# First projection of a two-layer decoder trunk as a fixed pipeline, with the later conditioning loads on GpSimd's queue

## The chip, the cores and the metric

The kernel runs on one core of one Trainium2 chip. The metric is the time of one execution on the device in microseconds (us). Three runs of the kernel before took 687.07, 687.56 and 693.68 us, with a median of 687.56.

## The reference

Two decoder layers work on x of 256 tokens by 1024 features, in float32. The vector c is passed through silu and multiplied by a 1024 x 6144 matrix of each layer (`ada_w`), which gives that layer's six conditioning vectors: shift, scale and gate for the mixer and for the feed-forward part. Cut to what matters here:

```python
mod = silu(c) @ ada_w[layer] + ada_b[layer]          # 6 vectors of 1024
h = rmsnorm(x, mix_pre_g[layer]) * (1.0 + scale_m) + shift_m
proj = h @ w_in                                       # layer 0: q, k, v of 16 heads
y = mixer(proj) @ w_out                               # layer 0 adds rel_bias to its scores
x = x + gate_m * rmsnorm(y, mix_post_g[layer])
h = rmsnorm(x, ffn_pre_g[layer]) * (1.0 + scale_f) + shift_f
u = causal_conv3(h @ w_up) + conv_b
y = (gelu(u_gate) * u_val) @ w_down
x = x + gate_f * rmsnorm(y, ffn_post_g[layer])
```

Layer 0 has eight softmax heads of kind A and eight of kind B, layer 1 eight latent heads (C) and eight stick-breaking heads (D).

## The kernel before

Every projection is computed in float32 quality from three products of float32r parts: a weight tile is loaded as it is (`raw`), ScalarE rounds it to a high part (L315) and VectorE subtracts that for a low part (L316). The activations are kept as `hh` and `hl` (features by tokens), and TensorE forms w_high·hh, w_low·hh and w_high·hl. So each weight passes DMA, ScalarE, VectorE and TensorE in turn.

The **first projection** (q, k and v of the A heads, 1024 x 1536 weights) runs over four slices of 256 input rows (`SLICES`). For a slice, `ada_first` multiplies silu(c) with the shift and scale columns of that slice alone (L154), ScalarE copies the sums out, four transposes (L232) turn them into columns, and three small VectorE operations (L235 to L238) finish the vectors A and B; then `h_part` writes `hh` (L367) and `hl` (L373) from transposed x, and the products L819 (q, k) and L323 to L325 (v) follow. The weights of `ada_first` are 2.1 MB a slice, those of the projection 1.57 MB. Tiles of tag `aw` (four of them, 512 KB each) hold conditioning weights, both for the slices and for everything later; tag `raw` has four tiles, tag `qkv` eight.

Behind the first projection the kernel forms the bias table of the scores (L830 to L838: a transpose, a product, an addition, a store to memory as `bias_d`), copies q, k and v out, and loads and turns the conv vectors `vec_b` (L851 to L857). Then come attention A, whose softmax (`soften`, L587) reads `bt` tiles loaded from `bias_d` (L864), the projection of the B heads (L477, L323 to L325), attention B, the output projection (y0m), a `boundary` with norms (m0), the feed-forward part, and layer 1 in the same manner. The remaining conditioning vectors are placed in this sequence by `ADA_AT`: kind "p" on TensorE (`ada_cols`, `ada_gate`), kind "v" on VectorE (`ada_vector`, two operations for each 512 KB tile), with the loads of each in `ada_load` (L143). The norms' reciprocal square roots (`rstd_halves`, L339 and L340), the masks of the D heads (L676) and some rotary arithmetic (L971, L972, L1025) are GpSimd's (POOL).

**Order.** A planner (`schedule_with_timeline_sim`) orders each engine's queue by simulated times, with program order as the priority. `manual_schedule` keeps the instructions of a block in written order on the engines named, but others may be planned between them; `issue_after(ins)` puts an instruction behind another on the same engine. Up to `in_order.close()` (L858) SyncE's (SP's) DMA issues stay in written order. An issue that waits for a free tile holds back what stands behind it in its queue.

Of the kernel before, what the change touches and what calls it, by code (L numbers as in the profile page):

```python
# [17 lines left out]
P = 128  # L18
# [47 lines left out]
def trunk_kernel(  # L66
# [70 lines left out]
    mods, last_load, last_gelu, last_full, last_h, last_down, last_low, last_main = {}, [], [], [], [], [], [], []  # L137

    def ada_load(layer, c0, tag="aw"):
# [18 lines left out]
    def ada_part(layer, c0, ws):  # L158
        ps = bank(f"ada_{layer}_{c0}", "a")
        ada_main(ps, ws)  # L160
# [59 lines left out]
    def ada_first(i, before=0, behind=0):  # L220
# [3 lines left out]
        if before:  # L224
            keep_clock(before)
# [14 lines left out]
    def ada_first_load(i, u):  # L240
        k0, n = SLICES[i]
        w = tl("aw", [P, 2, 512], f"aw_first{i}_{u}")
# [6 lines left out]
    def ada_gate(layer, which, h, post_g, tag="aw", on="a", on_vector=False):  # L249
# [22 lines left out]
        ada_main(ps, ws)  # L272
# [505 lines left out]
    first_ws = {0: [ada_first_load(0, u) for u in range(2)]}  # L778
# [4 lines left out]
    rb = small("rb", (16, 32), tag="o")  # L783
    oh = small("oh", (32, TW), tag="o")
    bias = small("bias", (16, TW), tag="o")
    for dst, src in ((rb, rel_bias), (oh, k_onehot), (bias, k_reach)):
        nc.sync.dma_start(dst, src)
    first_ws[0] += [ada_first_load(0, u) for u in range(2, 4)]
    vT = turned(vec_a, P, "vT")
    ada_first(0, 9, 6)  # L790
    w_in = ab_w_in[0]
    qkv = qkv_tiles("a")
    pq, pk = y_tile("psa_q"), y_tile("psa_k")
    pv = [bank(f"psa_v{t}") for t in range(2)]

    for i, (k0, n) in enumerate(SLICES):
        w = w_in[k0 * P:(k0 + n) * P]
        raw_qk = tl("raw", [P, n, 1024], f"rawaqk_{i}")
        for k in range(n):
            nc.sync.dma_start(raw_qk[:, k, :], w[k * P:(k + 1) * P, 0:1024])  # L800
# [294 lines left out]
```

## Time and profile before

| | |
|---|---|
| median of 3 runs | 687.56 us (687.07 to 693.68) |
| profiled execution | 689.92 us, of which the span of the trace is 687.9 us |
| TensorE (PE) busy | 660.6 us, 96% of the span; mean granted clock 0.99 |
| VectorE (DVE) busy | 524.7 us, 76% |
| ScalarE (ACT) busy | 369.0 us, 54% |
| GpSimd (POOL) busy | 33.9 us, 5% |
| moved by DMA | 159.10 MB, 231 GB/s in the mean |
| chain that ended last | PE 82%, DMA 5%, DVE 4%, ACT 4% |

The profiled execution is one run of the kernel, and every duration below is from it. The table's shares are means over stages with different limits; the stages are shown one by one further down. A granted clock of 1.00 is TensorE's full level of 2.4 GHz, and a stretch below 1.00 was spent partly at the lower one, 1.2 GHz.

### The profile page before, as it was taken

To read this page: it belongs to the slowest core of one execution; us is meant where nothing else is said; L and a number is where in the kernel's file an instruction comes from. 1 tells how busy PE (TensorE), PEld (TensorE's weight loads), DVE (VectorE), ACT (ScalarE), POOL (GpSimd) and SP (SyncE) were. 2 spreads that over 40 slices of the span, in tenths; PEclk is the share of its full clock that TensorE was granted. 3 is DMA by queue.
4 is the path that set the end of the run, shared out by engine and by line. 5 is a ranking of instruction groups with operands and counts; after the bars stand their busy time and mean duration, and the time that the engine had idled before them with its cause. 6 is when DMAs were issued, how large, how long until landed. Compare 5 with 4: busy or idle time off the path is not lost.

```text
span 687.9 us, 11772 instructions
## 1 busy us (share of the span) xinstructions
PE 660.6 (96%) x4547; PEld 571.4 (83%) x4547; DVE 524.7 (76%) x1008; ACT 369.0 (54%) x645; POOL 33.9 (5%) x95
## 2 busy tenths in 40 slices
PE   7899999799999999999999999989999999999996
PEld 5778976376899999999986998667599999999995
DVE  1545578688899999999898796764788777777775
ACT  3434365645565555555555645865565555555552
POOL 2000000001000000000002002410200000000000
PEclk9999999899999999999999999999999999999998
DMA  7899999986858778888885867723166555555511
GB/s 257 283 349 390 276 340 292 303 304 221 291 191 290 273 254 306 264 260 277 271 291 185 268 227 269 231 87 106 54 193 237 184 183 184 184 185 188 191 50 61
DMA packets 100818, 159.10 MB, mean 231 GB/s; under 512 B 4087, under 2 KB 62611, under 8 KB 100763
## 3 DMA queue, kind: packets, MB, share of 16 engines
q1 hardware_dynamic: 100739, 158.35, 69.5%
q8 instruction: 35, 0.57, 0.4%
q14 instruction: 20, 0.16, 0.1%
q10 hardware_dynamic: 24, 0.02, 0.0%
HBM read 156.52 MB, written 1.84 MB: 230 GB/s over the span
## 4 chain that ended last, share of the span: by engine, by line
PE 82%; DMA 5%; DVE 4%; ACT 4%; issue 2%; POOL 1%; SPq 1%; DVEq 0%; POOLq 0%; ACTq 0%
PE u L477 33%; PE y1f L698 9%; PE y0f L698 7%; PE psb L477 3%; PE psd L477 3%; PE y1m L698 2%; DMA aw<-in_ada_w 2%; PE psa_q L819 2%; PE psa_k L819 2%; DMA aw_first<-in_ada_w 2%; PE y0m L698 2%; PE ada L154 2%; DMA rawd<-in_ffn_w_down 1%; PE ada_first L154 1%; ACT junknm L335 1%
## 5 line engine op out<-in xcount | busy, mean ns | idle before, releaser
L747 ACT ACTIVATE cv<-u,cvT 128x256 f32<-128x256 f32 x88 | 49.1, 561 | 62.9 <-PE u L477 59.1
L477 PE MATMUL u<-hh,wu_0h 128*128 128x256 f32 x352 | 69.9, 280 | 1.2 <-DVE hh L431 1.2
L477 PE MATMUL u<-hh,wu_1h 128*128 128x256 f32 x352 | 70.1, 280 | 0.0
L477 PE MATMUL u<-hh,wu_1l 128*128 128x256 f32 x352 | 69.9, 279 | 0.0
L477 PE MATMUL u<-hh,wu_0l 128*128 128x256 f32 x352 | 69.5, 279 | 0.0
L315 ACT CAST wu_1h<-rawu 128x1024 fp32r<-128x1024 f32 x44 | 46.3, 1053 | 31.1 <-PE y1f L698 17.6
L748 DVE SCALAR_TENSOR_TENSOR cv<-u,cvT,cv 128x255 f32<-128x255 f32 x88 | 42.1, 479 | 26.4 <-ACT cv L747 26.3
L199 DVE SCALAR_TENSOR_TENSOR acc<-aw,cpad,acc 128x512 f32<-128x512 f32 x77 | 57.8, 751 | 2.0 <-DMA aw<-in_ada_w 1.6
L477 PEld LDWEIGHTS u<-hh,wu_0h 128*128 128x128 f32 x352 | 54.8, 188 | 4.2 <-PE ada L276 1.4
L316 DVE TENSOR_TENSOR wu_0l<-rawu,wu_0h 128x1024 fp32r<-128x1024 f32 x44 | 53.6, 1222 | 5.3 <-ACT wu_0h L315 5.3
L315 ACT CAST wu_0h<-rawu 128x1024 fp32r<-128x1024 f32 x44 | 46.0, 1046 | 19.0 <-PE u L477 19.0
L316 DVE TENSOR_TENSOR wu_1l<-rawu,wu_1h 128x1024 fp32r<-128x1024 f32 x44 | 53.7, 1220 | 3.0 <-ACT wu_1h L315 3.0
L477 PEld LDWEIGHTS u<-hh,wu_1l 128*128 128x128 f32 x352 | 53.7, 188 | 0.0
L477 PEld LDWEIGHTS u<-hh,wu_1h 128*128 128x128 f32 x352 | 53.7, 188 | 0.0
L477 PEld LDWEIGHTS u<-hh,wu_0l 128*128 128x128 f32 x352 | 53.5, 188 | 0.0
L477 PE MATMUL u<-hl,wu_1h 128*128 128x256 f32 x352 | 48.2, 279 | 0.0
L477 PE MATMUL u<-hl,wu_0h 128*128 128x256 f32 x352 | 48.2, 279 | 0.0
L315 ACT CAST wd_0h<-rawd 128x1024 fp32r<-128x1024 f32 x26 | 27.3, 1049 | 36.8 <-PE u L477 30.2
L477 PEld LDWEIGHTS u<-hl,wu_1h 128*128 128x128 f32 x352 | 44.2, 188 | 0.0
L477 PEld LDWEIGHTS u<-hl,wu_0h 128*128 128x128 f32 x352 | 44.2, 188 | 0.0
L316 DVE TENSOR_TENSOR wd_0l<-rawd,wd_0h 128x1024 fp32r<-128x1024 f32 x26 | 31.8, 1224 | 15.5 <-ACT wd_0h L315 15.3
L750 DVE SCALAR_TENSOR_TENSOR cv<-u,cvT,cv 128x254 f32<-128x254 f32 x88 | 41.9, 478 | 1.4
(556 smaller groups left out, 1547.5 us busy)
## 6 DMA issues: line engine op xcount, KB each, us to landing
rawu<-in_ffn_w_up SPq DMA_DIRECT2D x44, 1024.0 KB, 6.4
aw<-in_ada_w SPq DMA_DIRECT2D x80, 512.0 KB, 6.0
rawd<-in_ffn_w_down SPq DMA_DIRECT2D x22, 1024.0 KB, 5.6
aw_first<-in_ada_w SPq DMA_DIRECT2D x32, 256.0 KB, 5.1
rawaqk<-in_ab_w_in SPq DMA_DIRECT2D x8, 512.0 KB, 6.9
rawb<-in_ab_w_in SPq DMA_DIRECT2D x4, 1024.0 KB, 13.7
rawd<-in_cd_w_in SPq DMA_DIRECT2D x4, 1024.0 KB, 5.9
rawc<-in_cd_w_in SPq DMA_DIRECT2D x4, 544.0 KB
```

The source lines that it names most:

```text
L154: last_main[:] = [nc.tensor.matmul(ps[32 * j:32 * j + 32, 0:cols], cpad[:, k, :], ws[k // 2][:, k % 2, 0:cols], start=(n < 4), stop=(n >= ...
L199: nc.vector.scalar_tensor_tensor(acc, w, c_k, acc, op0=ALU.mult, op1=ALU.add)
L315: nc.scalar.copy(hi, src)
L316: low = nc.vector.tensor_tensor(lo, src, hi.bitcast(F32), op=ALU.subtract)
L335: nc.scalar.activation(junk, src, AF.Square, scale=D ** -0.5, accum_out=ss)
L477: nc.tensor.matmul(dst(f), w[:, k, f * P:(f + 1) * P], h[:, 4 * u + k, :], start=(u == 0 and first(f) and f not in seen), stop=(u == 1 and ...
L698: last_down[:] = [nc.tensor.matmul(ys[t][:, h, :], g[p // 2][:, t * P:(t + 1) * P], wu[p % 2][:, h * 512:(h + 1) * 512], start=start and p ...
L747: nc.scalar.activation(tt[:, s, :], u_ps, AF.Identity, bias=cvT[:, bcol:bcol + 1], scale=col(2))
L748: nc.vector.scalar_tensor_tensor(tt[:, s, 1:S], u_ps[:, 0:S - 1], col(1), tt[:, s, 1:S], op0=ALU.mult, op1=ALU.add)
L750: nc.vector.scalar_tensor_tensor(tt[:, s, 2:S], u_ps[:, 0:S - 2], col(0), tt[:, s, 2:S], op0=ALU.mult, op1=ALU.add)
L819: nc.tensor.matmul((pq, pk)[f // 4][:, f % 4 // 2, f % 2 * S:(f % 2 + 1) * S], w[:, f * P:(f + 1) * P], h[:, kk, :], start=(kk == 0 and f ...
```

## The change

The first projection's loads, and its work on TensorE, VectorE and ScalarE, are written out in one order, which these engines keep. All eight loads of slice 0's conditioning weights go ahead of the small vectors; those of slices 1 and 3 take `qkv` tiles. The bias table is formed in slice 1, the conv vectors are turned in slice 2, and the bias tiles of attention A are loaded inside the pipeline. All later conditioning products are queued behind the last product of the projection. The later conditioning loads, the four `gate` broadcasts and `rope` (L143, L256, L910 before: 80 + 4 + 1 DMAs) are issued by GpSimd, behind the last `rstd_halves` written before them. The products of "p" parts that are column vectors, and of layer gates with which == 2, run unbroken in the order of k 6, 7, 4, 5, 2, 3, 0, 1.

```diff
-    def turned(src, n, name):
-        ps = bank(f"ps_{name}", "a")
+    def turned(src, n, name, tag="a"):
+        ps = bank(f"ps_{name}", tag)
...
-            last_load[:] = [nc.sync.dma_start(
-                w, ada_w[layer, u * 256:(u + 1) * 256, c0:c0 + 512].rearrange("(k p) f -> p k f", p=P))]
+            with tc.issue_after(last_rstd[0].ins):
+                last_load[:] = [nc.gpsimd.dma_start(
+                    w, ada_w[layer, u * 256:(u + 1) * 256, c0:c0 + 512].rearrange("(k p) f -> p k f", p=P))]
...
-        with tc.manual_schedule(engines={mybir.EngineType.PE}) if at_once else nullcontext():
+        with ExitStack() as ctx:
+            if last_first:
+                ctx.enter_context(tc.issue_after(last_first[0].ins))
+            if at_once:
+                ctx.enter_context(tc.manual_schedule(engines={mybir.EngineType.PE}))
...
-        ada_main(ps, ws)
+        ada_main(ps, ws, at_once=True)
...
-    def ada_first(i, before=0, behind=0):
+    def ada_first(i, first=False):
...
-        ada_main(ps, first_ws[i], cols, i > 0)
-        nc.scalar.copy(part[:, 0:cols], ps[:, 0:cols])
-        if behind:
-            keep_clock(behind, last_main[0])
+        ada_main(ps, first_ws[i], cols, not first)
+        (nc.vector.tensor_copy if first else nc.scalar.copy)(part[:, 0:cols], ps[:, 0:cols])
+        yield
...
-        w = tl("aw", [P, 2, 512], f"aw_first{i}_{u}")
+        w = tl(("aw", "qkv")[i % 2], [P, 2, 512], f"aw_first{i}_{u}")
...
-                nc.sync.dma_start(mods[layer, which], post_g[layer:layer + 1, :].broadcast_to([P, D]))
+                nc.gpsimd.dma_start(mods[layer, which], post_g[layer:layer + 1, :].broadcast_to([P, D]))
...
-        nc.gpsimd.tensor_tensor(r, r, neg_half, op=ALU.pow)
+        last_rstd[:] = [nc.gpsimd.tensor_tensor(r, r, neg_half, op=ALU.pow)]
...
-    first_ws = {0: [ada_first_load(0, u) for u in range(2)]}
+    first_ws = {0: [ada_first_load(0, u) for u in range(4)]}
...
+    slice_load(0)
+    first_ws[1] = [ada_first_load(1, u) for u in range(4)]
...
+    for i in range(2):
+        nc.sync.dma_start(vec_b[i], cw[i * P:(i + 1) * P, :])
...
+    later_loads(1)
+    tabs_a = []
+
+    engines = {getattr(mybir.EngineType, e) for e in ("PE", "DVE", "Activation")}
+    with tc.manual_schedule(engines=engines):
+        keep_clock(9)
+        slice_x(0, range(1))
+        step = ada_first(0, True)
+        next(step)
+        slice_x(0, range(1, 2))
+        keep_clock(3)
+        vT = turned(vec_a, P, "vT", "g")
+        list(step)
+        wu = qk_split(0, 0)
+        slice_h(0)
+        for i in range(len(SLICES)):
+            more = i + 1 < len(SLICES)
+            qk_mm(i, 0, wu)
+            if i == 1:
+
+                ps = bank("ps_rb")
+                nc.tensor.transpose(ps[0:32, 0:16], rb, ident[0:16, 0:16])
+                rbT = const.tile([32, 16], F32, name="rbT")
+                nc.vector.tensor_copy(rbT, ps[0:32, 0:16])
+            if i == 2:
+                for m, v in enumerate(vec_b):
...
+                    nc.tensor.transpose(ps[:, m * P:m * P + n], v[:n, :], ident[:n, :n])
+            wu = qk_split(i, 1)
...
+            if more:
+                step = ada_first(i + 1)
+                next(step)
+            if i == 1:
+                ps = bank("ps_bias")
+                nc.tensor.matmul(ps[0:16, 0:TW], rbT, oh, start=True, stop=True)
+                nc.vector.tensor_add(bias, ps[0:16, 0:TW], bias)
+                later_loads(2)
+                nc.sync.dma_start(bias_d, bias[:, None, :].to_broadcast([16, 32, TW]))
+                later_loads(3)
+                tabs_a = [bias_tables(4 * g) for g in range(2)]
+            qk_mm(i, 1, wu)
+            wv = split(raw_v[i], [P, 2, 512], f"wav_{i}")
+            if more:
+                slice_x(i + 1)
+                list(step)
+                wu = qk_split(i + 1, 0)
+                slice_h(i + 1)
+            v_mm(i, wv)
...
-        nc.sync.dma_start(rope, k_rope)
+        nc.gpsimd.dma_start(rope, k_rope)
```

`slice_load(i)` issues a slice's two q/k loads and its v load, `later_loads(i)` that and then slice i + 1's conditioning loads. `slice_x` transposes x, `slice_h` is `h_part`, `qk_split` the split of one q/k tile, `qk_mm` its 24 products and `v_mm` the slice's 12 v products. `ada_first` is now in two steps: up to the copy, and the rest.

## Rows read from the trace of the kernel before

**Rows 1.** Busy time by stretch (us from the start of the span). Columns: length; busy us and instructions of PE, PE's weight load, DVE, ACT and POOL; mean granted TensorE clock; busy share of the DMA engines; GB/s moved.
```profile
0.00:13.00 13.00, 11.05 (x76) 9.60 (x76) 1.89 (x7) 5.39 (x12) 3.84 (x17) 1.00 0.74 236
13.00:20.76 7.76, 4.08 (x24) 2.15 (x25) 1.19 (x5) 2.48 (x3) 0.00 (x0) 1.00 1.01 344
20.76:25.60 4.84, 4.06 (x18) 3.71 (x19) 4.31 (x5) 1.95 (x3) 0.00 (x0) 0.65 1.09 365
25.60:36.00 10.40, 9.19 (x67) 6.85 (x65) 4.75 (x8) 3.64 (x4) 0.00 (x0) 1.00 0.64 217
36.00:47.00 11.00, 10.76 (x81) 8.98 (x82) 5.06 (x9) 4.37 (x6) 0.00 (x0) 1.00 1.01 355
47.00:69.00 22.00, 22.00 (x154) 17.49 (x152) 11.84 (x17) 9.89 (x15) 0.00 (x0) 1.00 1.04 382
69.00:87.00 18.00, 18.00 (x154) 17.38 (x154) 9.23 (x10) 6.12 (x7) 0.00 (x0) 1.00 1.00 270
...
120.00:131.30 11.30, 7.50 (x54) 3.90 (x54) 6.37 (x27) 7.84 (x22) 0.00 (x0) 1.00 1.08 310
131.30:138.50 7.20, 7.20 (x22) 3.98 (x23) 5.26 (x20) 4.11 (x16) 0.00 (x0) 0.53 0.93 304
138.50:162.00 23.50, 22.83 (x126) 17.03 (x125) 20.09 (x48) 9.86 (x22) 0.00 (x0) 1.00 0.89 301
180.00:350.00 170.00, 170.00 (x1253) 161.26 (x1252) 158.16 (x268) 93.22 (x125) 0.00 (x0) 1.00 0.82 273
420.00:460.00 40.00, 35.52 (x228) 27.78 (x228) 30.91 (x93) 30.24 (x70) 15.55 (x48) 1.00 0.52 166
```

**Rows 2.** Timeline of PE in the first projection. Columns: start us, us, engine, line, operation, out<-in, shapes, count; in brackets the idle time before it and what ended it.
```profile
16.33 1.05 PE L154 MATMUL ada_first<-aw_first,cpad 128*32 128x512 f32 x4 [1.65 <-DMA aw_first<-in_ada_w]
...
18.76 0.60 PE L232 MATMUL ada_first<-ident,part_first 128*128 128x128 f32 x4
20.76 0.48 PE L819 MATMUL psa_q<-hh,waqk_0h 128*128 128x256 f32 x2 [1.40 <-DVE hh L367]
...
22.25 0.58 PE L819 MATMUL psa_q<-hh,waqk_0l 128*128 128x256 f32 x1 [0.78 <-DVE waqk_0l L316]
...
36.02 0.39 PE L819 MATMUL psa_q<-hh,waqk_2h 128*128 128x256 f32 x1 [1.24 <-DVE hh L367]
```

**Rows 3.** Timeline of SP's DMA issues. A row spans its first to its last issue, so a long one held waits for free tiles.
```profile
2.19 2.06 SPq L244 DMA_DIRECT2D aw_first<-in_ada_w  x4
...
8.62 2.33 SPq L244 DMA_DIRECT2D aw_first<-in_ada_w  x4
...
12.58 8.06 SPq L244 DMA_DIRECT2D aw_first<-in_ada_w  x8
...
52.28 2.80 SPq L143 DMA_DIRECT2D aw<-in_ada_w  x4
...
63.85 0.68 SPq L838 DMA_DIRECT2D bias_d<-bias  x1
...
76.51 8.87 SPq L864 DMA_DIRECT2D bt<-bias_d  x8
```

**Rows 4.** The start of attention A: its first scores in PE's timeline, its first softmax operation in DVE's, and DVE's waits for the bias tiles (us in total, times, longest).
```profile
68.97 0.60 PE L579 MATMUL sab<-ka,qa 64*128 64x128 f32 x5
...
87.06 0.29 DVE L587 CUSTOM_DVE_ANT_0 ltab<-sab,bt 128x128 f32<-128x128 f32 x1 [1.86 <-DMA bt<-bias_d]
...
DVE ltab L587 <- DMA bt<-bias_d: 6.4, 2, 4.6
```

**Rows 5.** A late conditioning load: its issue in SP's timeline, its flight in the chain of waits, and the product that waited, in PE's timeline.
```profile
115.91 1.84 SPq L143 DMA_DIRECT2D aw<-in_ada_w  x3
...
121.03 10.22 DMA aw<-in_ada_w
...
131.30 1.92 PE L154 MATMUL ada<-aw,cpad 128*32 128x512 f32 x4 [3.08 <-DMA aw<-in_ada_w]
```

**Rows 6.** DMA issues by line: KB each, median us from issue to landing.
```profile
aw<-in_ada_w SPq DMA_DIRECT2D x80, 512.0 KB, 6.0
...
aw_first<-in_ada_w SPq DMA_DIRECT2D x32, 256.0 KB, 5.1
```

**Rows 7.** GpSimd and the loads of layer 1's attention: two rows of POOL's timeline, one of SP's, and PE's waits for POOL.
```profile
426.43 0.32 POOL L971 TENSOR_TENSOR qt<-rpq 128x64 f32<-128x64 f32 x1
426.71 0.77 POOL L972 TENSOR_TENSOR qt<-rpq 128x64 f32<-128x64 f32 x1
...
423.87 9.83 SPq L143 DMA_DIRECT2D aw<-in_ada_w  x4
...
PE sd L641 <- POOL spd L676: 0.7, 1, 0.7
```

**Rows 8.** Durations. First two rows of the page's groups (busy us, mean ns, idle before), then rows of the conditioning tiles (ns min/median/max, first and last start us).
```profile
L315 ACT CAST wu_1h<-rawu 128x1024 fp32r<-128x1024 f32 x44 | 46.3, 1053 | 31.1 <-PE y1f L698 17.6
...
L316 DVE TENSOR_TENSOR wu_0l<-rawu,wu_0h 128x1024 fp32r<-128x1024 f32 x44 | 53.6, 1222 | 5.3 <-ACT wu_0h L315 5.3
...
L154 PE MATMUL ada<-aw,cpad x144: 592/592/1061, 90.2 to 494.0; 128*32 128x512 f32 x144
L143 SPq DMA_DIRECT2D aw<-in_ada_w x80: 367/368/1314, 52.3 to 482.2; - x80
```

More of the change, by code (lines that the diff above doesn't have):

```diff
@@ L271, in ada_gate @@
         yield
-        ada_main(ps, ws)
+        ada_main(ps, ws, at_once=which == 2)
         yield
@@ L782, in trunk_kernel @@
     nc.sync.dma_start(vec_a[112:128, :], ffn_pre_g.rearrange("l (k p) -> (l k) p", p=P))
[L783 to L790, printed above, removed]
     w_in = ab_w_in[0]
-    qkv = qkv_tiles("a")
     pq, pk = y_tile("psa_q"), y_tile("psa_k")
@@ L794, in trunk_kernel, with slice_load @@
     pv = [bank(f"psa_v{t}") for t in range(2)]
[L796 removed]
+    raw_qk, raw_v = {}, {}
+    def slice_load(i):
+        k0, n = SLICES[i]
         w = w_in[k0 * P:(k0 + n) * P]
[L798 removed]
+        raw_qk[i] = tl("raw", [P, n, 1024], f"rawaqk_{i}")
         for k in range(n):
[L800 to L823 removed]
@@ new lines, in slice_load, with slice_x @@
+            nc.sync.dma_start(raw_qk[i][:, k, :], w[k * P:(k + 1) * P, 0:1024])
+        raw_v[i] = tl("raw", [P, n, 512], f"rawav_{i}")
+        last_slice[:] = [nc.sync.dma_start(raw_v[i], w[:, 1024:1536].rearrange("(k p) f -> p k f", p=P))]
+    def slice_x(i, ts=range(2)):
+        k0, n = SLICES[i]
+        if i not in slice_xT:
+            xb = bank(f"xTm0_{i}")
+            slice_xT[i] = {k: xb[:, (k - k0) * S:(k - k0 + 1) * S] for k in range(k0, k0 + n)}
+        for t in ts:
+            turn(slice_xT[i], t, list(slice_xT[i]), xns[t])
@@ new lines, in slice_h, with qk_split, qk_mm @@
+    def slice_h(i):
+        h_part(slice_xT[i], list(slice_xT[i]), slice(0, S), A, B, f"m0_{i}")
+    def qk_split(i, k):
+        return split(raw_qk[i][:, k, :], [P, 1024], f"waqk_{SLICES[i][0] + k}")
+    def qk_mm(i, k, wu):
+        kk = SLICES[i][0] + k
+        for w, h in ((wu[0], hh), (wu[1], hh), (wu[0], hl)):
+            for f in range(8):
+                nc.tensor.matmul((pq, pk)[f // 4][:, f % 4 // 2, f % 2 * S:(f % 2 + 1) * S],
+                                 w[:, f * P:(f + 1) * P], h[:, kk, :],
+                                 start=(kk == 0 and f % 2 == 0 and w is wu[0] and h is hh),
+                                 stop=(kk == KT - 1 and h is hl), skip_group_check=True)
@@ L824, in trunk_kernel, with v_mm @@
+    def v_mm(i, wu):
+        k0, n = SLICES[i]
         for k in range(n):
@@ L827, in trunk_kernel @@
                 tt = (slice(None), kk, slice(t * P, (t + 1) * P))
[L828 to L858 removed]
+                mm = mm3(pv[t], (hh[tt], hl[tt]), (wu[0][:, k, :], wu[1][:, k, :]), start=(kk == 0), stop=(kk == KT - 1))
+        if k0 + n == KT:
+            last_first[:] = [mm]
     def bias_tables(h0):
@@ L867, in bias_tables @@
         return t
+    slice_xT = {}
+    slice_load(0)
+    first_ws[1] = [ada_first_load(1, u) for u in range(4)]
+    rb = small("rb", (16, 32), tag="o")
+    oh = small("oh", (32, TW), tag="o")
+    bias = small("bias", (16, TW), tag="o")
+    for dst, src in ((rb, rel_bias), (oh, k_onehot), (bias, k_reach)):
+        nc.sync.dma_start(dst, src)
+    bias_d = dram.tile([16, 32, TW], F32, name="bias_d")
+    cvT = const.tile([P, 352], F32, name="cvT")
+    cw = ffn_conv_w.rearrange("l j (k p) -> (l j k) p", p=P)
@@ new lines, in trunk_kernel, with later_loads @@
+    vec_b = [small(f"vec_b{i}", (P, P), tag="o") for i in range(3)]
+    for i in range(2):
+        nc.sync.dma_start(vec_b[i], cw[i * P:(i + 1) * P, :])
+    nc.sync.dma_start(vec_b[2][0:8, :], cw[256:264, :])
+    nc.sync.dma_start(vec_b[2][8:96, :], ffn_conv_b.rearrange("l (k p) -> (l k) p", p=P))
+    def later_loads(i):
+        slice_load(i)
+        if i + 1 < len(SLICES):
+            first_ws[i + 1] = [ada_first_load(i + 1, u) for u in range(4)]
+    later_loads(1)
+    tabs_a = []
+    engines = {getattr(mybir.EngineType, e) for e in ("PE", "DVE", "Activation")}
@@ L869, in pairs_ab @@
+    qkv = qkv_tiles("a")
+    for half in range(2):
+        keep_feat(qkv[0], HD ** -0.5)(half, pq[:, half, :])
+        keep_feat(qkv[1])(half, pk[:, half, :])
+    keep_v(qkv[2], pv)
+    in_order.close()
     def pairs_ab(group, q, k, v):
-        tabs = [bias_tables(group * 8 + 4 * i) for i in range(2)]
+        tabs = [bias_tables(group * 8 + 4 * i) for i in range(2)] if group else tabs_a
         return [SoftmaxPair(head_rows(q, p), head_rows(k, p), head_values(v, p),
@@ L873, in pairs_ab @@
                             f"ab{group}_{p}", group * 4 + p, group * 4 + p in (1, 4, 6)) for p in range(4)]
-    gs = attend(pairs_ab(0, *qkv), "a")
+    pairs = pairs_ab(0, *qkv)
+    gs = attend(pairs, "a")
     qkv = qkv_proj(w_in, 1536, "b")
```

59 lines of the change are left out of this document (6 added, 53 removed).

## The prediction

> **What bounds the kernel now.** I read the page first: TensorE is busy 96% of the span and makes 82% of the chain that ended last, so only stretches where it stands or runs at its lower clock can give anything. The busy times by stretch say where these are [rows 1]. The feed-forward part (180 to 350 us) has none: TensorE is busy for 170.00 of 170 us, and VectorE for 158.16. What is left in the stages that the change touches lies in three places.
>
> First, the start. The first product of the projection runs at 20.76 us, and the timeline ahead of it shows why [rows 2]: TensorE waits for the last slice-0 conditioning tile until 16.33 us, then the sums are copied, turned and worked into vectors. SP's timeline shows why that tile is late [rows 3]: only half of its loads go out at 2.19 us, the rest at 8.62 us behind six small loads.
>
> Second, the projection itself, from 20.76 to 69.0 us, 48.24 us long. Idle in it are 0.78 + 1.21 + 0.24 = 2.23 us, and in its first 4.84 us the granted clock is 0.65, which costs about 4.06 x 0.35 = 1.4 us [rows 1]. So it holds 48.24 - 2.23 - 1.4 = 44.6 us of work.
>
> Third, the end of the attentions. At 128 us TensorE waits 3.08 us for a conditioning tile that took 10.22 us to land [rows 5]; from 120 to 162 us it is idle for 3.80 + 0.67 us, and after the wait it works 7.20 us at a clock of 0.53, a loss of 3.4 us [rows 1]. Together 7.9 us. Behind this lies attention A: its first scores are ready at 69 us, its softmax starts at 87.06 us, since the bias table is stored at 63.85 and its tiles are issued from 76.51 us [rows 3, 4].
>
> The DMA engines matter beside TensorE: their share is 0.94 to 1.08 through most of 36 to 131 us, but 0.74 up to 13 us and 0.64 from 25.6 to 36 us [rows 1], where SP stood 8.06 us with a run of eight issues before it [rows 3].
>
> **The change, part by part.**
>
> *Start.* Slice 0 needs x (1.05 MB) and 2.10 MB of conditioning. In 13 us the chip moved 236 x 13 = 3.07 MB, then 344 GB/s [rows 1], so with all eight loads ahead the last lands at about 13.3 us, 3 us sooner. After it: 1.05 us of products [rows 2], a copy of about 0.5, the transposes 0.60 [rows 2] and three small operations of about 0.6 (an estimate: the transposes end at 19.36, the first product follows at 20.76 us, and half a us to 0.8 of that is `hh`) make 16.1 us. The written order then puts the low part of the first weight ahead of `hh`. That weight is complete at 3.74 MB, about 14.9 us; rounding 1.05 and subtracting 1.22 [rows 8] make 17.2, and half a us of `hh` 17.8 us. I take the first product at 17.8, 3.0 us sooner.
>
> *The first hand-over.* TensorE now follows a written order: after 24 products it needs all of slice 1's conditioning tiles, and nothing fills a wait. They end at 1.05 + 2.10 + 0.06 + 1.57 + 2.10 = 6.88 MB, so at 13 + 3.81/0.344 = 24.1 us. The 24 products last about 4.5 us if they start at the low clock as they do now, to 22.3 us. So TensorE stands 1.8 us, the eight conditioning products of 1.9 us end at 26.0, and of 44.6 us of work about 4.7 are done.
>
> *The rest of it.* The three turns of the conv vectors move in (0.8 us, an estimate; they are taken from the next stage, so they cost nothing in all, and I leave them out of both). 26.0 + 39.9 = 65.9 us; three hand-overs where VectorE must finish vectors, a low part of 1.22 and `hh` within the 2.8 us of v products cost about 0.5 each: 67.5. ScalarE's copy, `qkv` tiles for odd slices and the later loads' place cost nothing here: SP no longer waits for `aw` tiles.
>
> *GpSimd's loads in the middle.* The first later group, 2.1 MB, is free to leave once slice 2's `aw` tiles are used, near 38 us instead of 52.28 [rows 3], and then shares the DMA engines with slice 3. At 355 GB/s [rows 1] it is 5.9 us of transfer. Bounds: 0 if slice 3 is ahead by then, 5.9 if all of it delays slice 3. I take 2.5, nearer to 0, because slice 3's conditioning is needed at about 48 us and would land near it. The projection ends at 70.0 us, **+1.0** against 69.0.
>
> The Trainium skill ("DMA: Bandwidth & Descriptors", Issuing engines are not separate DMA queues) speaks against this move: loads issued by different engines run on the same 16 DMA engines and interleave, so a second queue saves issue time only. By that rule the term would be 5.9; no row here shows two such streams together.
>
> *After it.* Bias tiles would be there when the scores are, so softmax A starts 17 us sooner. TensorE is full from 69 to 120 us anyway [rows 1], so nothing is won at once; but attention A ends earlier, its `aw` groups are used and reloaded earlier, and the load that came at 131.25 us [rows 5] leaves earlier. Queueing all later conditioning products behind the projection costs nothing: the first of them ran at 90.2 us [rows 8]. The unbroken order, which begins with the tile loaded last, costs 0 to 3.1 us a group [rows 5]; 0 if loads come earlier. Of 7.9 us I take 6 (bounds 0 and 7.9): **-6.0**.
>
> *85 DMAs on GpSimd.* No row shows a DMA issued there. Bounds for one issue: 0.37 and 1.31 us, SP's median and longest [rows 8]; even 85 x 1.31 = 111 us fit beside 34 us of work. In the feed-forward part six groups, 24 tiles, are needed in some 150 us, about 6 us for each, against a landing of 6.0 [rows 6] with four tiles in flight, so 0. At boundary m0 the gate loads stand shortly before the norms: **+0.5** (0 to 1.5). In layer 1's attention TensorE has 4.48 us of idle in 420 to 460 us and waits for GpSimd's masks now and then [rows 1, 7]: five more issues of 0.37 to 1.31 us between them are 1.9 to 6.6 us, of which about half can lie on the chain; **+1.0**. A gain from SP's freed queue I put at 0: what was waited for after 69 us is conditioning and bias tiles [rows 4, 5].
>
> **Sum:** 1.0 - 6.0 + 0.5 + 1.0 = -3.5 us on the profiled 689.92 (span 687.9 and 2.0 around it), 686.4. The median of the runs lies 2.4 lower, at 687.56, so the forecast is 684.0 us.
>
> **The rivals.**
>
> *B, more comes back.* DMA runs at the 382 GB/s of 47 to 69 us [rows 1] already from 13 us: the first hand-over is 1.1 us sooner, slice 3 isn't delayed (2.5), one us less in hand-overs and layer 1 each, and all 7.9 are won (1.9 more): 7.5 less, 676.5 us. For it: 365 GB/s beside the first products [rows 1]. Against: slices' conditioning comes in 1 KB pieces, and 344 to 355 was seen with them.
>
> *C, slower: GpSimd's queue holds up the masks.* At 423.87 us SP issues four loads and stands 9.83 us over them for free tiles [rows 7]. On GpSimd the same wait stands in front of the masks of the D heads, on which the chain runs, if the planner's times put these loads first. Price: 9.83 + 5 x 0.37 = 11.7 in place of the 1.0: 694.7 us. It decides from the point where GpSimd waits longer than the masks can spare, about 1 us. Against: the planner orders by times that know of the tiles.
>
> Beside it the Trainium skill ("SBUF — State Buffer", SBUF: two separate sides) warns that GpSimd cannot write descriptors while VectorE holds their shared port. Here one operation beside VectorE took 0.77 us, its like 0.32 [rows 7]. With that section's figures, 0.62 and 3.1 us, five loads would lose some 12 us, an estimate from the page; that would be much the same price.
>
> *D, nothing left.* The 2.1 MB interleave fully with slice 3, 3.4 us more: 687.4, within noise of before, or the planner sets the loads so that the late one is only another. For it: a DMA share at 1.0 [rows 1].
>
> **How the numbers follow.** Forecast 46%, with a range of its own of 679 to 690; B 22%, C 18%, D 14%. About 1% (6.9 us) is what a measurement can tell from no change: faster is below 680.7, slower above 694.4. Faster: B 22 and a quarter of the forecast's 46, together 34%. Slower: C, 18%. Within: 48%. The range from 675 to 697 takes in B and C with their bounds and leaves out about 15%.
>
> **What would show it.** Right: the first projection product near 17.8 us; no run of SP issues held for 8 us before 36 us; softmax A at about 70; no 3 us wait near 131 and a clock of 1.00 there; GpSimd's loads as a DMA queue of their own; masks in layer 1 no later than now against the products before them. Wrong: TensorE standing for `aw_first` or raw tiles of slices 1 to 3 by more than 4 us in all; masks whose releaser is a DMA issue; VectorE's sums waiting for `aw` in the feed-forward part, which I cost at nothing, and where its 11.84 us of slack in 170 [rows 1] would go first.

## The result and the profile after

The changed kernel takes **697.48 us** in the median of four runs (696.89 to 698.94); the kernel before took 690.62 on the same chip, in the median of four runs (one of them, at 1086.69 us, was disturbed and is left out of the ratio). The ratio is 1.0124, with an interval of 1.0082 to 1.0166. The forecast was 684.0 in a range of 675 to 697: the change is slower by over 1%, on the other side of the forecast. The profiled execution took 697.84 us (span 695.9), 7.92 more than the 689.92 of before.

Where the time went is seen first at three fixed points. Each boundary begins with a norm whose first operation runs on GpSimd; here are the first of layer 0's mixer, of its feed-forward part and of layer 1's mixer, in POOL's timeline of the kernel before:
```profile
162.88 0.30 POOL L339 TENSOR_SCALAR rpm<-sspm 128x1 f32<-128x1 f32 x1 [152.34 <-ACT junkpm L335]
...
360.66 0.30 POOL L339 TENSOR_SCALAR rpf<-sspf 128x1 f32<-128x1 f32 x1 [187.90 <-ACT junkpf L335]
...
485.16 0.30 POOL L339 TENSOR_SCALAR rpm<-sspm 128x1 f32<-128x1 f32 x1 [30.12 <-ACT junkpm L335]
```
and in that of the changed kernel:
```profile
170.85 0.30 POOL L342 TENSOR_SCALAR rpm<-sspm 128x1 f32<-128x1 f32 x1 [5.25 <-ACT junkpm L338]
...
368.23 0.30 POOL L342 TENSOR_SCALAR rpf<-sspf 128x1 f32<-128x1 f32 x1 [15.65 <-ACT junkpf L338]
...
492.87 0.30 POOL L342 TENSOR_SCALAR rpm<-sspm 128x1 f32<-128x1 f32 x1 [5.50 <-ACT junkpm L338]
```
The differences are 7.97, 7.57 and 7.71 us. So all of the loss arises before the first norm; the feed-forward part and layer 1 add nothing. The rest of this section looks at those 170 us. Busy time by stretch, columns as in [rows 1]:
```profile
13.00:17.80 4.80, 2.45 (x18) 1.45 (x14) 3.23 (x8) 1.05 (x1) 0.00 (x0) 1.00 1.05 374
17.80:36.00 18.20, 16.37 (x109) 14.18 (x109) 7.75 (x13) 6.40 (x9) 0.00 (x0) 0.91 0.93 299
36.00:47.00 11.00, 10.25 (x71) 7.94 (x72) 4.57 (x9) 3.31 (x5) 3.68 (x5) 1.00 1.05 377
47.00:55.00 8.00, 2.91 (x25) 2.52 (x27) 2.44 (x3) 1.13 (x2) 0.00 (x0) 0.84 1.03 334
55.00:73.90 18.90, 18.90 (x120) 14.90 (x112) 10.30 (x14) 9.13 (x12) 0.00 (x0) 0.89 0.93 266
...
87.00:130.20 43.20, 43.20 (x310) 33.42 (x308) 27.44 (x59) 21.24 (x41) 8.67 (x12) 1.00 0.79 281
130.20:143.00 12.80, 1.45 (x7) 0.93 (x6) 11.07 (x33) 5.17 (x19) 2.17 (x3) 0.66 1.07 296
143.00:150.00 7.00, 7.00 (x31) 5.08 (x31) 6.72 (x28) 4.49 (x14) 1.45 (x2) 0.64 1.08 365
...
188.00:358.00 170.00, 170.00 (x1253) 161.21 (x1253) 160.10 (x272) 93.94 (x127) 21.38 (x30) 1.00 0.82 272
```
TensorE loses time at two places: 5.09 us in 47 to 55 us, with a lower clock behind it, and 11.35 us in 130 to 143, after which it works 7 us at a clock of 0.64. PE's timeline names both:
```profile
17.80 0.78 PE L818 MATMUL psa_q<-hh,waqk_0h 128*128 128x256 f32 x4 [2.35 <-DVE hh L370]
...
23.12 1.45 PE L160 MATMUL ada_first<-aw_first,cpad 128*32 128x512 f32 x9 [0.73 <-DMA aw_first<-in_ada_w]
...
36.75 2.04 PE L160 MATMUL ada_first<-aw_first,cpad 128*32 128x512 f32 x16 [1.85 <-DMA aw_first<-in_ada_w]
...
54.57 3.75 PE L160 MATMUL ada_first<-aw_first,cpad 128*32 128x512 f32 x16 [5.09 <-DMA aw_first<-in_ada_w]
...
127.50 0.39 PE L328 MATMUL psb_v<-wbv_1h,hl 128*128 128x512 f32 x1
...
139.11 1.09 PE L177 MATMUL ada<-ident,acc 128*128 128x128 f32 x4 [8.85 <-DVE acc L205]
142.71 3.11 PE L604 MATMUL sab<-ident,ltab 128*128 128x128 f32 x12 [2.51 <-DVE ltab L601]
```
The first stand is for slice 3's conditioning. Its loads and those of the first later group meet, as the issues of SP and of POOL show; the second block is the last of slice 3's loads in the chain of waits, in flight for 13.86 us where the median of these loads is 6.6:
```profile
33.64 7.30 SPq L247 DMA_DIRECT2D aw_first<-in_ada_w  x8
...
38.12 3.12 POOL L145 DMA_DIRECT2D aw<-in_ada_w  x4 [27.74 <-PE ada_first L160]
...
121.11 2.89 POOL L145 DMA_DIRECT2D aw<-in_ada_w  x4 [10.61 <-PE ada L160]
...
122.18 0.37 SPq L311 DMA_DIRECT2D rawu<-in_ffn_w_up  x1
122.60 12.44 SPq L837 DMA_DIRECT2D bt<-bias_d  x8
```
```profile
40.58 13.86 DMA aw_first<-in_ada_w
```
The second stand is before attention B. In VectorE's timeline its softmax (L590) comes after seven of the eight sums (`acc`) of conditioning group (0,4,1); eight heads of attention A come first, the ninth head is B's:
```profile
78.13 0.29 DVE L590 CUSTOM_DVE_ANT_0 ltab<-sab,bt 128x128 f32<-128x128 f32 x1 [0.17 <-PE sab L584]
...
105.99 0.29 DVE L590 CUSTOM_DVE_ANT_0 ltab<-sab,bt 128x128 f32<-128x128 f32 x1
...
125.66 0.49 DVE L207 TENSOR_SCALAR acc<-aw,cpad 128x512 f32<-128x512 f32 x1 [3.51 <-DMA aw<-in_ada_w]
...
133.93 1.53 DVE L205 SCALAR_TENSOR_TENSOR acc<-aw,cpad,acc 128x512 f32<-128x512 f32 x2
137.10 0.29 DVE L590 CUSTOM_DVE_ANT_0 ltab<-sab,bt 128x128 f32<-128x128 f32 x1 [1.64 <-DMA bt<-bias_d]
```
The kernel before had it the other way round, softmax B from 123.72 us and the sums behind three of its four pairs:
```profile
123.72 0.28 DVE L587 CUSTOM_DVE_ANT_0 ltab<-sab,bt 128x128 f32<-128x128 f32 x1
...
135.50 0.48 DVE L201 TENSOR_SCALAR acc<-aw,cpad 128x512 f32<-128x512 f32 x1
```
So softmax A starts 8.9 us sooner (78.13 against 87.06 in [rows 4]) and softmax B 13.4 us later. Three candidates for the later one stand in these rows: the sums ahead of it, whose loads leave at 121.11 us; its tables, issued from 122.60 and landed at 137; and TensorE's order, since the second projection's v products end at 127.50 where they ended at 114.07, attention A's products having gone ahead of them. Nothing else fills TensorE meanwhile: the output projection `y0m` starts only behind B's first value products, at 135.35 us before and at 147.22 after (in the kernel's text it takes the banks of tag `y`, where B's first and third pair keep their scores).

### The profile page after: what moved, and what is told of

It reads as the page before. It is cut to its first block, busy times and chain, and to the rows that moved or that the text cites. A ratio compares the mean times of both kernels' runs of the same rounds, so it can differ in the third digit from the quotient of the medians.

```text
span 695.9 us, 11779 instructions
## 1 busy us (share of the span) xinstructions
PE 658.0 (95%) x4541; PEld 573.1 (82%) x4541; DVE 526.7 (76%) x1007; ACT 368.6 (53%) x644; POOL 95.2 (14%) x180
## 4 chain that ended last, share of the span: by engine, by line
PE 80%; DMA 9%; DVE 4%; ACT 3%; POOL 1%; issue 1%; SPq 0%; DVEq 0%; POOLq 0%; ACTq 0%
PE u L480 35%; PE y1f L701 9%; PE y0f L701 8%; DMA aw_first<-in_ada_w 5%; PE psb L480 3%; PE psd L480 3%; PE y0m L701 2%; PE y1m L701 2%; DMA rawav<-in_ab_w_in 2%; DMA bt<-bias_d 2%; PE ada L160 1%; PE sab L604 1%; PE ada_first L160 1%; ACT junknm L338 1%; PE sab L613 1%
## 5 line engine op out<-in xcount | busy, mean ns | idle before, releaser
L145 POOL DMA_DIRECT2D aw<-in_ada_w x80 | 58.2, 729 | 333.1 <-DVE acc L205 181.6
```

Of the source, the lines that this page charges most:

```text
L145: last_load[:] = [nc.gpsimd.dma_start(w, ada_w[layer, u * 256:(u + 1) * 256, c0:c0 + 512].rearrange("(k p) f -> p k f", p=P))]
```

## The experiments

Times are medians, each with the ratio to the kernel before on the same chip and its interval. The runs were made on several chips, so kernels are compared by their ratios. Places inside a kernel (a start, a stand) are from one profiled execution of each.

**GpSimd's loads in the kernel before** (the 85 loads as in the change, the rest as before):
```diff
-            last_load[:] = [nc.sync.dma_start(
+            with tc.issue_after(last_rstd[0].ins):
+                last_load[:] = [nc.gpsimd.dma_start(
```


> The kernel before with one part of the change alone: the 85 conditioning, gate and rope loads are issued by GpSimd behind the first norm's multiplier; the pipeline, its table tiles and the orders behind the projection stay as they were. Theory of the order (TensorE's planned queue puts all of attention A ahead of the second projection, because in the pipeline A's scores are ready before that projection starts): the queue of before stays, A's last two pairs still stand among and behind the second projection's v products, so it gives 687 to 693 us, within 0.7% of before, with less than 9 us of idle TensorE at 115 to 160 us. Rival (GpSimd's loads land late and themselves make the hole): it gives 695 to 700, and TensorE stands over 10 us at 115 to 160.

689.91 us, 0.9988 [0.9952, 1.0023], as the theory of the order had it. In this profile the late load of [rows 5] is nearly gone and the first norm comes at 158.70 us:
```profile
125.94 1.05 PE L156 MATMUL ada<-aw,cpad 128*32 128x512 f32 x4 [0.85 <-DVE stab L599]
```
In this kernel GpSimd's queue costs no time. In the medians the wait's 3 us don't show; the profiled execution, at 685.48 us, was the second shortest of ten and 4.4 us below their median, so its early norm need not be typical of the kernel.

**The loads back on SP, in the changed kernel** (the three edits undone, `nc.gpsimd` to `nc.sync`):

> The changed kernel with its 85 later conditioning loads back on SP's queue; the pipeline is kept. Theory I (the loads' place: GpSimd's first group overtakes slice 3's conditioning on the DMA engines): that group now stands behind slice 3's conditioning in one queue, so the wait of 5.1 us for it falls below 2 us and the low clock after it (2.3 us) goes; but slice 3's raw weights stand behind the group's 2.6 MB. End of the first projection 69 to 72 us instead of 73.9, whole kernel 690 to 695 us. Rival II (the written order itself is too tight for the DMA, whoever issues): the wait stays at 4 us or more, whole kernel 696 or above.

699.21 us, 1.0115 [1.0072, 1.0157]. Slice 3's stand is replaced by one of 5.71 us at 65.69, for `hh` of slice 3, and the last product of the projection starts at 75.22 (73.61 in the changed kernel). Here too the sums of group (0,4,1), all eight, run ahead of softmax B, which starts at 140.46. The time is in rival II's range, by another wait than the one it named. The loss does not go with the queue.

**The first later group behind slice 3** (group (0,2,0) and its gate on SP behind `last_slice`):
```diff
-            with tc.issue_after(last_rstd[0].ins):
-                last_load[:] = [nc.gpsimd.dma_start(
+            early = (layer, c0) == (0, 2 * D)
+            with tc.issue_after((last_slice if early else last_rstd)[0].ins):
+                last_load[:] = [(nc.sync if early else nc.gpsimd).dma_start(
```


> The changed kernel with the first later group alone (four loads and one gate broadcast, 2.6 MB) on SP's queue behind slice 3's last load; the other 80 loads stay on GpSimd. Theory I: the 5.1 us wait falls to 1 us or less, the clock stays at 1.00 behind it, the projection ends at 66 to 68 us, and if the attentions keep their length the kernel takes 689 to 691 us. Rival II: the wait stays above 3 us. Rival III (only the end of attention B counts, where the tables are late): the projection ends earlier but the time stays at 695 to 698.

699.28 us, 1.0104 [1.0048, 1.0159]. The stand before slice 3 is gone, though its loads leave SP as in the changed kernel (32.98 to 40.27 us here, 33.64 to 40.94 there), so the 2.1 MB were its cause. The projection's last product starts at 65.53 in place of 73.61, 8.1 us earlier. But the time doesn't follow; it lies above even rival III's 698. The stretches after it:
```profile
20.00:65.50 45.50, 43.06 (x307) 35.58 (x306) 22.59 (x35) 16.41 (x22) 0.00 (x0) 1.00 1.01 315
65.50:80.00 14.50, 11.39 (x56) 6.80 (x55) 5.45 (x11) 5.92 (x10) 3.12 (x4) 0.76 1.01 363
80.00:130.00 50.00, 50.00 (x360) 39.53 (x360) 31.72 (x83) 28.46 (x63) 8.68 (x12) 1.00 0.84 286
130.00:150.00 20.00, 8.36 (x40) 6.05 (x37) 18.72 (x62) 9.10 (x32) 4.34 (x6) 0.66 1.01 327
```
From 65.5 to 80 us TensorE stands 3.11 us (the next weights, `rawb`, are late) and loses 11.39 x 0.24 = 2.7 by the clock; from 130 it stands 11.64, as in the changed kernel. What was won is lost by the end of the second wait: the first norm comes at 171.14.

**Attention B's tables ahead of the up weights:**
```diff
-                raws.append(load(w_up[:, c0:c0 + 256], KT, 256, f"rawu{name}_{s}"))
+                with tc.issue_after(last_table[0].ins) if (layer, b) == (0, 0) else nullcontext():
+                    raws.append(load(w_up[:, c0:c0 + 256], KT, 256, f"rawu{name}_{s}"))
```


> The changed kernel with the first two feed-forward weight loads of layer 0 queued behind the bias tables of attention B on SP (nothing else). Theory: TensorE's 8.8 us wait near 130 us is VectorE's softmax B standing for tables that SP issues only from 122.6 us, behind a weight load that waits for a tile: tables issued from 116 to 118, softmax B from about 130.5 us, the wait falls to 4 us or less, the kernel takes 690 to 693 us. Rival (the wait is for the conditioning sums on VectorE, whose weights land late): softmax B starts earlier, the wait stays above 7 us and the time at 696 or more.

697.82 us, 1.0101 [1.0065, 1.0136], as the rival had it. The tables are issued from 115.35 to 120.35 us, and softmax B still starts only at 134.81, with VectorE busy on sums and weight parts until then:
```profile
126.15 0.49 DVE L207 TENSOR_SCALAR acc<-aw,cpad 128x512 f32<-128x512 f32 x1 [5.14 <-DMA aw<-in_ada_w]
...
134.81 0.29 DVE L590 CUSTOM_DVE_ANT_0 ltab<-sab,bt 128x128 f32<-128x128 f32 x1
```
The tables alone aren't the cause, though the chain of waits of the changed kernel named them: the other wait ends at nearly the same time. With the first group moved as well (the last two edits together):

> Both edits: the first later group behind slice 3 on SP, and the first feed-forward loads behind the tables of attention B. If the two stands are separate costs, their gains add: 684 to 687 us, below the kernel before. If one stand only hands its time to the other, the result is that of the better single edit, 689 to 692.

700.0 us, 1.0139 [1.0087, 1.019], beyond both expectations; softmax B at 136.27, a stand of 11.21 us.

**The sums behind softmax B:**
```diff
-    "bv": [("v", 0, 4, 1)],
+    "b1": [("v", 0, 4, 1)],
...
+                with tc.issue_after(last_soft[0].ins) if behind else nullcontext():
+                    nc.vector.tensor_scalar_mul(acc, w, c_k)
```


> The changed kernel, with VectorE's conditioning sums of group (0,4,1) held behind the third pair of attention B's softmax, where the planned queue of the kernel before has them (the changed kernel's queue has seven of the eight ahead of the first pair). TensorE's order and the loads stay. Theory of VectorE's queue (softmax B stands behind sums whose loads land at 125 to 136 us): softmax B starts as soon as its tables land, 133 to 136 us instead of 137.1, the last of its four pairs' chain is 3 to 5 us earlier, first norm at the boundary 166 to 169 instead of 170.9, total 693 to 695. Rival of TensorE's order (attention A's products are spent before the second projection ends, so the chain of B runs bare): the wait only changes its name, total 696 to 699.

695.74 us, 1.0068 [1.0045, 1.0092]. The time lies between the two expectations. Now it is the tables that softmax B waits for, and it wins 1.1 us:
```profile
135.99 0.29 DVE L592 CUSTOM_DVE_ANT_0 ltab<-sab,bt 128x128 f32<-128x128 f32 x1 [3.98 <-DMA bt<-bias_d]
```
**Both, sums behind and tables first:**

> As the run before, and attention B's bias tables loaded ahead of the first up weights of the feed-forward (they land near 120 us). Theory of VectorE's queue: nothing is left ahead of softmax B but its scores, which end at 128 to 129; softmax B starts at 128 to 131, idle TensorE at 125 to 150 us falls from 11.4 to under 5, first norm at the boundary 162 to 166, total 688 to 692. Rival of TensorE's order: with nothing to fill, TensorE still stands 8 us or more while VectorE and ScalarE do the first pairs, total 694 to 698.

692.43 us, 1.0016 [0.9986, 1.0046], at the edge of the expected 692. Softmax B starts at 130.03, 7.1 us sooner than in the changed kernel, the stand is 5.37 in place of 11.36 us, and the first norm comes at 165.40:
```profile
130.03 0.28 DVE L592 CUSTOM_DVE_ANT_0 ltab<-sab,bt 128x128 f32<-128x128 f32 x1
...
137.19 0.48 DVE L209 TENSOR_SCALAR acc<-aw,cpad 128x512 f32<-128x512 f32 x1
```
```profile
135.04 2.87 PE L607 MATMUL sab<-ident,ltab 128*128 128x128 f32 x12 [5.37 <-DVE ltab L604]
```
The four kernels make a square. Softmax B starts at 137.10 us with neither edit, 134.81 with the tables, 135.99 with the sums and 130.03 with both: 2.3 and 1.1 us alone, 7.1 together. Two waits lay side by side in front of it, and each hid a good part of what the other was worth there. The ratios are 1.0124, 1.0101, 1.0068 and 1.0016: only the kernel with both edits is clear of the changed one, and that the gains in time do more than add is not shown. The 6.3 us that are left of the 13.4 go with TensorE's order: B's first scores come only at 127.22 here, and at 114.40 in the kernel before.

**The order put into the kernel before** (softmax B's first pair behind the fourth sum, nothing else):
```diff
+                with tc.issue_after(last_sum[0].ins) if name == "ab1_0" else nullcontext():
+                    nc.vector.tensor_tensor_reduce(out=lt[:, cols], in0=ps[:, cols], in1=tt, scale=-1.0,
```


> The kernel before, with the first pair of softmax B held behind the first four of the sums of group (0,4,1), the order that the changed kernel's queue has; nothing else is touched. Their loads, behind SP's others, landed at 131 to 137 there. Theory of VectorE's queue: softmax B starts at 133 to 138 instead of 123.7, TensorE stands 5 us or more there, first norm at the boundary 166 to 172 instead of 162.9, total 693 to 699. Rival (that order is harmless by itself): under 1% of change, 688 to 692, and first norm at 161 to 165.

700.03 us, 1.0145 [1.0111, 1.0179], a little beyond the expected 699. The second projection still ends early, its last product at 112.78 us, and softmax B stands behind the sums all the same. But it isn't the sums' loads that the queue waits for here. Ahead of them the planner has now set the reduction `mod` of another group, whose products on TensorE wait for the late load of [rows 5] until 129.86; the sums then run without a wait:
```profile
133.69 0.17 DVE L172 TENSOR_REDUCE mod<-ada 128x4 f32<-128x16 f32 x1 [7.48 <-PE ada L171]
...
133.98 0.48 DVE L203 TENSOR_SCALAR acc<-aw,cpad 128x512 f32<-128x512 f32 x1
134.50 2.33 DVE L201 SCALAR_TENSOR_TENSOR acc<-aw,cpad,acc 128x512 f32<-128x512 f32 x3
136.74 0.28 DVE L590 CUSTOM_DVE_ANT_0 ltab<-sab,bt 128x128 f32<-128x128 f32 x1
```
```profile
129.86 1.92 PE L154 MATMUL ada<-aw,cpad 128*32 128x512 f32 x4 [3.73 <-DMA aw<-in_ada_w]
...
142.27 1.59 PE L604 MATMUL sab<-ident,ltab 128*128 128x128 f32 x6 [8.69 <-DVE ltab L601]
```
In the kernel before, that `mod` came at 140.07, behind three pairs of softmax B. So operations on late loads, set ahead of softmax B in VectorE's queue, make a loss of the size of the change's in a kernel that has none of its other parts. The load that was waited for is another than in the changed kernel, so the run shows what such an order costs and not the same wait.

**TensorE's order.** Three runs put it to the test. Attention A's tables loaded after the pipeline:

> The changed kernel, but attention A's bias tables are loaded where the kernel before loads them, when the pairs are set up after the pipeline, and not inside it. Theory of the order: A's softmax starts later, some of A's products move back among and behind the second projection, but its last pair still comes before the last v product; the hole at 130 to 145 us shrinks by 1 to 5 us, total 693 to 697. Rival (the late conditioning sums make the hole): nothing at 130 to 145 changes, total 697 to 699.

701.74 us, 1.0157 [1.0107, 1.0206]: softmax A at 82.47, softmax B at 138.13, a stand of 13.26 us. Both expectations missed: a later attention A made it worse, and the sums' first load came later too, at 131.73. Attention A's last two pairs behind the second projection:
```diff
-    gs = attend(pairs, "a")
+    gs = []
+    steps = attend_steps(pairs, gs, "a")
+    for _ in range(3):
+        next(steps)
     qkv = qkv_proj(w_in, 1536, "b")
+    list(steps)
```


> The changed kernel, with attention A's last two pairs written behind the second projection (and the two conditioning groups that follow them moved to behind its k half, so that their loads keep their turn). Theory of the order: TensorE gets back some 5 us of A's products behind the last v product while attention B's first softmax runs on VectorE; the second projection ends 4 to 6 us earlier, at 121 to 124 us, idle TensorE at 115 to 150 falls from 11.4 to under 7, the first norm at the boundary comes at 164 to 167 instead of 170.9, total 691 to 694. Rival (VectorE's queue, with the conditioning sums that wait for late loads ahead of softmax B): softmax B still starts at 135 to 140, idle stays at 10 to 13, total 697 to 700.

696.32 us, 1.0108 [1.0069, 1.0146]. The time falls between the two expectations. The v products end 8.7 us sooner, at 118.77, more than expected, and it helps little, since VectorE's queue stands at the sums with A's last head behind them:
```profile
129.65 0.49 DVE L207 TENSOR_SCALAR acc<-aw,cpad 128x512 f32<-128x512 f32 x1 [6.50 <-DMA aw<-in_ada_w]
```
And attention B's first scores ahead of the v products:

> The changed kernel, with the first scores of attention B written ahead of the second projection's v half instead of behind it. Theory of the order: softmax B's first pair can run on VectorE and ScalarE under the 48 v products; the first softmax B comes at 118 to 127 us, the hole at 130 to 145 shrinks by 4 to 8 us, total 690 to 694. Rival (VectorE's queue and late loads): the tables of B land at 135 in any case and the first softmax B stays at 135 to 138, so nothing is won, total 697 to 700.

695.89 us, 1.0064 [1.0038, 1.0089]. The first pair's softmax runs at 115.24, the second only at 134.42, behind the same sums. The time lies between the expectations; 1.6 us are won by the medians, and by the ratios its interval still touches the changed kernel's.

**Combinations.** All edits on VectorE's side, and the scores first:

> As the run before, and attention B's first scores ahead of the second projection's v half. Both theories together (the queue of VectorE and the order of TensorE): the first softmax B at 114 to 119 us under the v products, idle TensorE at 115 to 150 under 3, first norm at the boundary 159 to 163, total 684 to 689. If only one of the two matters, it equals the run before, or the run with the scores alone (696).

693.85 us, 1.0053 [1.002, 1.0086]. TensorE's stand at 130 us is down to 0.88 and 0.56, but one of 3.35 for the sums has come at 146.24, and the first norm is at 165.53 as without the scores. So it equals the run before, as was expected if only one of the two theories matters. With the first group behind slice 3 too:

> As the run before, and GpSimd's first conditioning group and the first gate loaded by SP behind the pipeline's last slice (that edit alone ended the projection at 65.5 us instead of 73.9, and lost it again at 130 to 150). If what ends the stage is VectorE's queue and the tables, and both are free now, the 8 us earlier end of the projection is kept in part (2 to 3 us go for the weights of the second projection that come late at 72): first norm at the boundary 153 to 160, total 678 to 685. Rival (something else, as the chain of late conditioning loads, ends the stage whatever precedes it): the same as the run before, within 1.5 us.

693.75 us, 1.0053 [1.0023, 1.0082], the rival's "the same": the projection's last product starts at 67.61, earlier than the 68.64 of the kernel before, and the first norm still comes at 166.70. And the sums, the tables and the later pairs:

> The changed kernel with three edits together: the sums of group (0,4,1) behind the third pair of softmax B, attention B's tables ahead of the first up weights (these two alone gave 692.4), and attention A's last two pairs behind the second projection (alone 696.3, where VectorE stood 6.5 us for the sums' loads). If the order of TensorE costs what is left over the kernel before with GpSimd's loads (first norm at the boundary 165.4 against 158.7): the 48 v products end at 117 to 120, softmax B starts at 119 to 124, idle TensorE at 115 to 150 under 4 us, first norm at 159 to 162, total 684 to 689. If only VectorE's queue mattered: the same as the two edits, 691 to 694.

700.66 us, 1.0159 [1.0128, 1.0191], against an expected 684 to 689 or 691 to 694: the v products end at 119.39, but softmax B starts at 129.81, 0.2 us sooner than without the pairs moved, since A's last head (127.05) now stands ahead of it, and the first norm comes at 170.06. So the run doesn't bear out that TensorE's order is what remains; as softmax B came no sooner, it doesn't rule it out either.

**The start, in the kernel before** (GpSimd's loads, and all eight loads of slice 0 at once):
```diff
-    first_ws = {0: [ada_first_load(0, u) for u in range(2)]}
+    first_ws = {0: [ada_first_load(0, u) for u in range(4)]}
```


> The kernel before with the two parts of the change that cost nothing alone: GpSimd's loads (alone 689.9), and the first slice's four conditioning loads issued together, ahead of the vectors (the prediction's term of 3.0 us). First product of the projection at 17.8 to 18.5 us instead of 20.8; if that is kept to the end, total 686 to 688; if the DMA engines, which are 96% busy at 20 to 70 us, take it back, 689 to 691.

689.05 us, 0.9983 [0.9958, 1.0009]. The first product is at 21.08, not at 18. The loads do leave earlier, but the vector loads now stand behind them: TensorE waits until 13.54 for `vec_a`, and the sixteen conditioning products, which come behind its turn, run in one piece for 3.38 us at a clock of 0.55, to end no sooner than before:
```profile
13.54 0.30 PE L112 MATMUL ps_vT<-ident,vec_a 128*128 128x128 f32 x1 [2.45 <-DMA vec_a<-in_ffn_pre_g]
14.23 3.38 PE L156 MATMUL ada_first<-aw_first,cpad 128*32 128x512 f32 x16 [0.38 <-DVE vT L114]
```
In the changed kernel the written order puts the turn of `vec_a` behind these products, at 14.74.

## Why the prediction was wrong

| step | predicted | measured |
|---|---|---|
| first product | 17.8 us | 17.80 |
| first hand-over | a wait of 1.8 | 0.73 |
| end of the projection | 70.0, +1.0 | 73.9, +4.9 |
| softmax A | about 70, 17 us sooner | 78.13, 8.9 sooner |
| from there to the first norm | -6.0 and +0.5 | +3.1 (96.95 against 93.88 us) |
| layer 1 | +1.0 | 0 |
| profiled time | -3.5 | +7.92 |

**The step that failed is the one after the projection, "Of 7.9 us I take 6".** It held that attention A's earlier end would reload the conditioning tiles earlier and so take the late load of [rows 5] away. That came true as far as it went: softmax A ran 8.9 us sooner, and the group that waited until 131.30 us ran at 119.74 without a wait:
```profile
119.74 1.92 PE L160 MATMUL ada<-aw,cpad 128*32 128x512 f32 x16
```
What it didn't follow is the next group, (0,4,1), which VectorE sums. Its loads leave at 121.11 us, not yet landed when softmax B is due, and in the planned queue of the changed kernel its sums stand ahead of softmax B instead of behind it. The bounds, 0 and 7.9, had no loss in them: the step took the wait of before as the most that could be at stake, where a queue that waits in order can also grow a new one. Idle and lost clock in this stage are 11.35 + 1.45 x 0.34 + 7.00 x 0.36 = 14.4 us (130.2 to 150 us), against 7.9. The stage is only 3.1 us longer, so by this sum some 3 us of TensorE's work have left it; the turns of the conv vectors and the bias table's product went into the projection, and the rest I didn't trace.

Shown is the cause of most of this loss: with the sums behind softmax B and its tables early, the ratio falls from 1.0124 to 1.0016, and the medians leave 2.3 us against the kernel before (692.43 and 690.12). In the kernel before, an order with late conditioning work ahead of softmax B costs 10 us. Not shown is why the planner turned the order round. GpSimd's loads alone didn't do it, and with the loads back on SP it stayed turned, so it goes with the rest of the change, the pipeline and the orders behind it.

**The second step is a size: the 2.5 us "in the middle".** The mechanism was named, the first later group sharing the DMA engines with slice 3, and the run without it confirms it; the group left at 38.12 us, as forecast. But it was sized as transfer time. It measured 5.09 us of standing, and 3.75 us, at a granted clock of 0.50, for products that take 2.04 at the full clock. The bound of 5.9 was passed once this clock is counted (5.09 + 1.7 = 6.8), and by the run without it the projection ends 8.1 us sooner. The Trainium skill ("DMA: Bandwidth & Descriptors", Issuing engines are not separate DMA queues) says that loads issued by different engines interleave on the same DMA engines. The trace agrees: slice 3's last load took 13.86 us beside GpSimd's. With the whole 5.9 us for the term the sum would have been 3.4 us nearer; but taking the sharing away won no time at the end, so this step alone doesn't explain the result.

**Rival D** had much of the truth: the two streams interleaved, and the late load was "only another". It priced that second half at nothing won, 687.4, where the other load cost more than the one it replaced. **Rival C**, the one on the slower side, put its price on the wrong engine and stage: in layer 1 TensorE waits 2.0 us for the masks in place of 0.7 [rows 7], and nothing of it reaches the end. The 0.77 us against 0.32 that it set beside VectorE don't bear on it: VectorE was at work beside both operations. Of **rival B** one term came true in this profile, the first hand-over 1.1 us sooner (0.73 in place of 1.8, with 374 GB/s in 13 to 17.8 us); in the profile of the run with the first group behind slice 3 it was 1.79, and the rest of B didn't come.

The base of the sum was low as well: the 2.4 us by which the forecast went below the profile came from three runs, where 17 to 31 runs of the kernel before on other chips have medians of 690.0 to 690.2.

What held: the first product to a hundredth of a us, and with its path (the last conditioning tile at 12.81 against 13.3, the low part done at 17.19 against 17.2), though the hundredth itself is luck (and the "eight conditioning products of 1.9 us" are sixteen, of 2.04); the feed-forward part, TensorE full for 170.00 of 170 us beside VectorE's 160.10 with the loads on GpSimd; boundary m0 and layer 1 as good as free. "VectorE's sums waiting for `aw` in the feed-forward part" was on the list of what would prove it wrong; they did so, but one stage earlier, where I hadn't looked. "TensorE standing for `aw_first`" by more than 4 us in all was on it too: 0.73 + 1.85 + 5.09 = 7.7 us.

**Open** is why the pipeline's kernel doesn't get below the kernel before with both waits out of the way. Its first norm is at 165.40, against 162.88 in the kernel before and 158.70 in that kernel with GpSimd's loads (a profile 4.4 us below its median). Of the 6.7 us to the latter, 4.7 are there when the projection ends (last product at 73.01 against 68.36). Yet neither the first group moved, nor the scores, nor the pairs brought it nearer: each opened another wait. No version that was run beats the kernel before by more than it can be measured.

## What to carry to other kernels

When a change makes one stage ready earlier, read the planned order of every in-order queue behind it anew: an operation whose data comes by DMA, placed ahead of the critical chain in such a queue, turns a load's lateness into everybody's. Give "what becomes of a wait" a bound on the side of loss too. And where a wait is named by its last releaser, look for the second one beside it before pricing its removal: here each fix alone moved softmax B by 1 to 2 us, and both together by 7.

## What the runs showed of the hardware

A load of 512 KB costs GpSimd 0.72 us to issue, twice SP's 0.37 [rows 8], and lands as fast: 6.2 us in the median, where SP's took 6.0 [rows 6]. The page's issues and the line's durations (ns min/median/max):
```profile
aw<-in_ada_w POOLq DMA_DIRECT2D x80, 512.0 KB, 6.2
```
```profile
L145 POOL DMA_DIRECT2D aw<-in_ada_w x80: 707/724/938, 38.1 to 486.6; - x80
```
The longest issue of 80 took 0.94 us, though VectorE was 94% busy beside 28 of them (160.10 of 170 us). The Trainium skill ("SBUF — State Buffer", SBUF: two separate sides) warns of a trap in which VectorE keeps GpSimd from writing a load's descriptors, so that the load takes 3.1 us in place of 0.62. No such lengthening shows here; most of VectorE's work here is of forms with two inputs, and which forms would bring it on was not tried.
